# Forget logits, V's summed operands and the fourth merged splits in another order, and one gate pair computed earlier

## The chip, the cores and the metric

The kernel runs on one core of a Trainium2 chip. The metric is the device time of one execution in microseconds. TensorE (PE) multiplies, VectorE (DVE) and ScalarE (ACT) work on tiles, GpSimd (POOL) and SyncE (SP) issue DMAs here.

## The reference

One layer on x of 512 x 2048, in fp32. A normalized input is projected, three branches of attention with four heads of 128 each run on the projection, and their outputs are gated, merged and projected again:

```python
hn = rmsnorm(x, norm_g)
proj = jnp.einsum('bsd,dc->bsc', hn, w_in)        # q, k, v, SiLU gate of three branches; forget logits; merge gates
ya = forgetting_attention(qa, ka, va, f_logit)    # branch A, f_logit = 4 columns of proj + b_f
yb = chunked_relpos_attention(qb, kb, vb, rel_bias)   # branch B
yc = stick_breaking_attention(qc, kc, vc)         # branch C
ys = jnp.stack([ya, yb, yc], axis=2) * jax.nn.silu(gate)
up = jnp.einsum('bsnw,nwd->bsnd', ys, w_up)
merged = jnp.sum(sigmoid(merge_gates) * up, axis=2)
return x + jnp.einsum('bsd,de->bse', merged, w_out)
```

In branch A the forget logits go through log-sigmoid and a cumulative sum, and the differences are added to the attention logits.

## The kernel before

Every fp32 operand of a product is split in two: ACT copies it into a type of lower precision (the high part, L249) and DVE subtracts that copy to get the rest (the low part, L253). The projections then run in units of 16 matmuls on PE (L268), eight with 512 columns and eight with 256, and each unit has one tile of weights, which SP loads as `raw` and which ACT and DVE split into `w`. There are six `raw` buffers and three of `w`.

To save multiplications, blocks of the projection are computed by a scheme of seven products in place of eight, of sums of operands: products 1, 2, 6, 5, 7, 3, 4 in this order. The sums of weights are made in two ways: POOL issues a load that adds to a tile already there (L293), and DVE adds two tiles (L662, L668, and L903 for V). A pair task computes one block of q and k columns, of SiLU gates ("s"), or of merge gates ("g", a gate pair) in seven units. A value task ("v") computes the V columns of one branch in 14 units, each named (p, kh) by its product p and its half kh of the contraction. Its operands of product 1 and 5 are summed into that of product 6 (L903), and those of 2 and 6 into that of product 3. Results are gathered from the accumulators by ACT (L742, L746, L763) and DVE (L735, L750, L767, L778, L789).

The branches run as C, B, A. The first head of C has code of its own (its columns, the V task of branch C, a gate pair). For each later head the table HEADS (L1951) lists what PE computes right behind that head's q and k columns. The "v" at C's fourth head (C, 3) is V of branch B, and the "v" at B's fourth is V of branch A. In this document the three are the first, second and third V task. The heads' own softmax work lies on ACT and DVE between the splits. Small operands of attention are transposed by DMAs on SP (L281 with `tt`).

The order of everything is written out by a planner in the kernel (class Flow, L65). A task is a generator that yields an engine, a cost and, where given, a due time; the planner keeps a clock for each engine and picks the task that can start first, and among such the one due first. It runs when the program is built, and what it picks becomes the fixed order of PE, ACT, DVE, SP and POOL. So a number in a table or a due time changes the order of instructions, and each engine then works its list from the front: an instruction whose input isn't there holds all behind it.

The four places that the change touches:

- `forget_bias` (L963): the forget logits of branch A are computed early, in four partial sums, stored, loaded back as `lf_parts` in another layout by SP (L281), summed by DVE (L978), and put through some fifteen small operations (L979 to L999) with one exponential on ACT (L983). The result goes back to memory, to be loaded for the heads of branch A.
- The value task's loop over loads (L883): it sets the order in which SP loads V's weights. The loads of product 5 get POOL's accumulating load behind them. The order also shifts when DVE may make the sums (L903).
- `merged_d` (L1664): the merged output is split for the last projection in four groups m1 to m4; the fourth, `m4`, has due times of its own.
- HEADS.

Of the kernel before, what the change touches and what calls it, by code (L numbers as in the profile page):

```python
# [29 lines left out]
HS = S // 2  # L30
# [5 lines left out]
A, B, C = 0, 1, 2  # L36
# [28 lines left out]
class Flow:  # L65
# [16 lines left out]
    def give(self, slots, n=1):  # L82
        slots.free += [self.fin] * n

    def spawn(self, gen, slack, ready=None):
        task = Task(gen, slack, self.now if ready is None else ready)
        self.tasks.append(task)
        self.advance(task)
# [66 lines left out]
def act_us(n, x=1):  # L155
    return x * (0.075 + 0.00095 * n)


def dve_us(n, x=1):
    return x * (0.1 + 0.00105 * n)  # L160
# [3 lines left out]
def hybrid_kernel(  # L164
# [33 lines left out]
    flow = Flow()  # L198
# [4 lines left out]
    def t2(s, dt=F32):  # L203
        return tp.tile([P, S], dt, tag="t2", name=nm(s))
# [11 lines left out]
    def f(ap):  # L216
        return ap.bitcast(F32)
# [4 lines left out]
    LH, RH = slice(0, HS), slice(HS, S)  # L222
# [23 lines left out]
    def split(hi, lo, src, n, ev=None, due=(), hi_ev=None):  # L246

        yield (ACT, act_us(n), *due)
        nc.scalar.activation(hi, src, AF.Copy)  # L249
        if hi_ev is not None:  # L250
            set_(hi_ev)
        yield (DVE, dve_us(n), *due)
        nc.vector.tensor_sub(lo, src, f(hi))  # L253
        if ev is not None:
            set_(ev)
# [17 lines left out]
    def landing(issued, kb):  # L273

        line[0] = max(line[0], issued + 1.0) + kb / RATE
        return line[0] + 1.5

    def queued(dma, to, src, us=0.4):

        yield SP, us  # L280
        tc.keep_in_program_order(dma(to, src))  # L281

    def fetch(to, src, kb):
        yield from queued(nc.sync.dma_start, to, src)
        return Event(landing(flow.fin, kb))
# [11 lines left out]
    def added(there, begun, parts):  # L297

        yield begun
        for to, src, kb in parts:  # L300
            ev = yield from add_up(to, src, kb)
        there.t = ev.t
# [84 lines left out]
    def raw_tile(shape=(UK, P)):  # L387
        return wp.tile([P] + list(shape), F32, tag="raw", name=nm("raw"), bufs=NR)
# [230 lines left out]
    class PairTask:  # L619
# [24 lines left out]
        def load(self):  # L644
            a11, a12, a21, a22 = self.src
            for p, srcs in ((5, (a21, a22)), (1, (a11,)), (2, (a12,)), (7, (a11, a21)), (4, (a22,))):
                yield raws, 1
                t = self.w[p] = raw_tile()
                ev = yield from fetch(t, srcs[0], 512)
                if len(srcs) > 1:  # L650
                    spawn(added(self.there[p], ev, [(t, srcs[1], 512)]), 0.0, flow.fin)
                else:
                    self.there[p].t = ev.t
            self.w[6], self.w[3] = self.w[1], self.w[2]
# [165 lines left out]
    class ValueTask:  # L820
# [34 lines left out]
        def load(self):  # L855
            def src(i, kh):
                return w_v[self.n, i // 2, i % 2, kh]

            def begin(p, kh):
                if p == 7:  # L860
                    yield t2s, 2
                    self.w[p, kh] = [t2("raw").rearrange("p (j c) -> p j c", j=2) for _ in range(2)]
                else:
                    yield raws, 1
                    self.w[p, kh] = raw_tile((UK // 2, 2 * P))
                for to, c in pieces(p, kh):
                    w, kb = src({5: 2, 1: 0, 2: 1, 7: 0, 4: 3}[p], kh)[:, c], 128 * (c.stop - c.start)
                    if p == 7:
                        yield POOL, 0.8
                        tc.keep_in_program_order(nc.gpsimd.dma_start(to, w))  # L870
                        ev = Event(landing(flow.fin, kb))
                    else:
                        ev = yield from fetch(to, w, kb)
                if p in (5, 7):
                    more = [(to, src({5: 3, 7: 2}[p], kh)[:, c], 128 * (c.stop - c.start)) for to, c in pieces(p, kh)]
                    return lambda: spawn(added(self.there[p, kh], ev, more), 0.0, flow.fin)
                self.there[p, kh].t = ev.t

            def pieces(p, kh):
                w = self.w[p, kh]  # L880
                return [(w, slice(0, 4))] if p != 7 else [(t, slice(2 * i, 2 * i + 2)) for i, t in enumerate(w)]

            for p, kh in ((1, 0), (1, 1), (5, 0), (2, 0), (2, 1), (5, 1)):  # L883
                add = yield from begin(p, kh)
                if p == 5:
                    add()
            adds = []
            for kh in range(2):
                adds.append((yield from begin(7, kh)))
            for add in adds:  # L890
                add()
            for kh in range(2):
                yield from begin(4, kh)
# [69 lines left out]
    f_ev, f2_ev = Event(), Event()  # L963
    fd, fd2 = dp.tile([NQ * NH, S], F32, name="fd"), dp.tile([NH, S], F32, name="fd2")

    def forget_bias():

        T = S // 32
        lf = cp.tile([P, 4 * T], F32, name="lf")
        parts = cp.tile([P, NQ, T], F32, name="lf_parts")  # L970
        v, u, s, p = (lf[:, i * T:(i + 1) * T] for i in range(4))
        yield f_ev
        yield from queued(nc.sync.dma_start, parts,
                          fd.rearrange("(n h) (c t) -> n (h c) t", h=NH, t=T).rearrange("n c t -> c n t"))
        yield Event(f_ev.t + 12.0)
        q = 0.21
        yield DVE, 2 * q
        nc.vector.tensor_reduce(v, parts.rearrange("p n t -> p t n"), axis=AX.X, op=ALU.add)  # L978
        nc.vector.tensor_scalar_add(v, v, bfc)  # L979
        yield DVE, q  # L980
        nc.vector.scalar_tensor_tensor(u, v, -1.0, v, op0=ALU.mult, op1=ALU.min)
        yield ACT, q
        nc.scalar.activation(u, u, AF.Exp)  # L983

        yield DVE, 5 * q
        nc.vector.tensor_scalar_add(s, u, 2.0)
        nc.vector.reciprocal(s, s)
        nc.vector.tensor_mul(s, s, u)
        nc.vector.tensor_mul(u, s, s)
        nc.vector.tensor_scalar_mul(p, u, 1.0 / 17.0)  # L990
        for k in range(7, 0, -1):
            yield DVE, q
            nc.vector.scalar_tensor_tensor(p, p, 1.0 / (2 * k + 1), u, op0=ALU.add, op1=ALU.mult)
        yield DVE, 3 * q
        nc.vector.scalar_tensor_tensor(p, p, 1.0, s, op0=ALU.add, op1=ALU.mult)
        nc.vector.tensor_scalar_mul(p, p, 2.0)
        nc.vector.scalar_tensor_tensor(v, v, 0.0, p, op0=ALU.min, op1=ALU.subtract)
        yield from queued(nc.sync.dma_start, fd2.rearrange("h (c t) -> (h c) t", t=T), v)
        f2_ev.t = flow.fin + 3.0  # L999
# [474 lines left out]
    def first_head(n, h):  # L1474
        hd = Head(n, h)
        units.extend(first_quad(hd))
        at(OFF["fb"], forget_bias, 20.0)
        value_units(n)
        gate_units()
        schedule(hd, OFF["a0"], OFF["b0"])  # L1480

    def head(n, h, more, last=False):
        hd = Head(n, h, last)
        u0 = len(units)
        units.extend(PairTask(col(n, Q, h), col(n, K, h), ops, hd.got(Q), None, hd.got(K)).units)
        for i, what in enumerate(more):
            if what == "v":
                value_units(n - 1)
            elif what == "s":
                units.extend(PairTask(col(n, G, h), col(n, G, h + 1), ops, hd.got(G), None, far(n, h + 1)).units)  # L1490
            else:
                gate_units(x1_first=last and i == len(more) - 1)
        schedule(hd, u0 + 7, u0 + 21)
        return hd

    first_head(C, 0)
    for n, h, more in HEADS:
        last_head = head(n, h, more, (n, h) == (A, NH - 1))
# [107 lines left out]
    kept_m, m1_ev, up_half, up_done = {}, [Event() for _ in range(UK)], Event(), Event()  # L1606
# [47 lines left out]
    def merged_d(k, b):  # L1654

        yield up_done
        for i in range(UK):
            yield lambda: m23[i] is not None
        if k % 2 == 0:
            yield xps, 1  # L1660
            m4[k // 2] = Parts("m4")
        yield lambda: m4[k // 2] is not None
        h, lo, ev = m4[k // 2].half(k % 2)
        yield from split(h, lo, b[:, RH], HS, ev, (up_done.t + 10.0 + k,))  # L1664
        give(t2s)

    QK = UK // 4
# [265 lines left out]
    for k in range(UK):  # L1933
# [12 lines left out]
NX = 28  # L1946
NR = 6

XLATE, SLOW, RATE = 6.0, 3.0, 330.0
ONTO = {6: 1, 7: 6, 4: 7, 3: 5}  # L1950
HEADS = [(C, 1, "gg"), (C, 2, "sg"), (C, 3, "v"), (B, 0, "sggg"), (B, 1, "g"), (B, 2, "sggg"),  # L1951
         (B, 3, "gvg"), (A, 0, "sgg"), (A, 1, "gg"), (A, 2, "sggg"), (A, 3, "gggg")]

OFF = dict(cs=3, ct=12, s=11, t=17, v=1, av=8, s1=8, t1=13, v1=0, av1=3, fb=24, a0=11, b0=23)
# [55 lines left out]
```

## Time and profile before

| | before |
|---|---|
| median of 3 runs | 1295.91 us (1294.97 to 1295.99) |
| profiled execution | 1296.0 us |
| its span | 1294.3 us |
| granted TensorE clock | 1.000 |
| PE busy | 1286.4 us, 99% |
| DVE busy | 1137.5 us, 88% |
| ACT busy | 873.6 us, 67% |
| POOL busy | 100.0 us, 8% |

The span reaches from the first to the last instruction; 1.7 us lie outside it. A busy share is the mean over the span. A group's row gives its line in the kernel, the engine, the operation, output and inputs by name, the shape, and the count. Brackets behind a row give the idle time in front of it and whose end ended it.

### The profile page before, as it was taken

To read this page: it belongs to the slowest core of one execution; us is meant where nothing else is said; L and a number is where in the kernel's file an instruction comes from. 1 tells how busy PE (TensorE), PEld (TensorE's weight loads), DVE (VectorE), ACT (ScalarE), POOL (GpSimd) and SP (SyncE) were. 2 spreads that over 40 slices of the span, in tenths; PEclk is the share of its full clock that TensorE was granted. 3 is DMA by queue.
4 is the path that set the end of the run, shared out by engine and by line. 5 is a ranking of instruction groups with operands and counts; after the bars stand their busy time and mean duration, and the time that the engine had idled before them with its cause. 6 is when DMAs were issued, how large, how long until landed. Compare 5 with 4: busy or idle time off the path is not lost.

```text
span 1294.3 us, 19472 instructions
## 1 busy us (share of the span) xinstructions
PE 1286.4 (99%) x6965; PEld 1113.1 (86%) x6965; DVE 1137.5 (88%) x1667; ACT 873.6 (67%) x1359; POOL 100.0 (8%) x130
## 2 busy tenths in 40 slices
PE   9999999999999999999999999999999999999998
PEld 6888888888888888888888888888888888888887
DVE  8988889888898999989889989999899877798775
ACT  8877677778767769666867675967768655454432
POOL 0200001010110101002010000000100000000000
PEclk9999999999999999999999999999999999999999
DMA  9778798887889869889897888888979755774831
GB/s 333 232 203 217 205 233 200 210 205 194 232 228 198 236 189 220 243 190 246 203 230 209 187 229 223 210 233 190 234 203 278 239 194 195 214 235 136 247 112 65
DMA packets 130257, 274.47 MB, mean 212 GB/s; under 512 B 43104, under 2 KB 49504, under 8 KB 130160
## 3 DMA queue, kind: packets, MB, share of 16 engines
q1 hardware_dynamic: 113504, 217.19, 53.7%
q0 software_dynamic: 16224, 55.58, 25.5%
q8 instruction: 55, 0.90, 0.3%
q10 hardware_dynamic: 432, 0.45, 0.1%
q14 instruction: 42, 0.34, 0.1%
HBM read 241.54 MB, written 24.42 MB: 205 GB/s over the span
## 4 chain that ended last, share of the span: by engine, by line
PE 93%; DVE 4%; DMA 1%; issue 1%; ACT 1%; SPq 0%; ACTq 0%
PE acc L268 74%; PE att L268 14%; DVE w L253 1%; DMA sg<-gl 1%; DVE m L253 1%; PE att L264 1%; PE att L1322 1%; PE att L1323 1%; PE att L265 1%; PE att L263 1%; PE att L1321 1%; DVE sg L1586 0%; ACT w L249 0%; DMA raw<-in_w_one 0%; PE att L1435 0%
## 5 line engine op out<-in xcount | busy, mean ns | idle before, releaser
L253 DVE TENSOR_TENSOR w<-raw,w 128x1024 fp32r<-128x1024 f32 (+2 forms) x432 | 499.9, 1165 | 94.0 <-ACT w L249 93.5
L249 ACT ACTIVATE w<-raw 128x1024 fp32r<-128x1024 f32 (+2 forms) x432 | 435.2, 1011 | 216.8 <-PE att L268 106.6
L268 PE MATMUL acc<-x,w 128*128 128x512 f32 (+1 forms) x2656 | 499.7, 339 | 1.5 <-ACT v L746 1.1
L268 PEld LDWEIGHTS acc<-x,w 128*128 128x128 f32 x2656 | 424.7, 189 | 66.9 <-issue 3.4
L268 PE MATMUL acc<-t,w 128*128 128x512 f32 (+1 forms) x1920 | 357.5, 338 | 0.7 <-DVE v L767 0.7
L268 PEld LDWEIGHTS acc<-t,w 128*128 128x128 f32 x1920 | 292.6, 190 | 34.5 <-DVE v L767 0.9
L293 POOL DMA_DIRECT2D raw<-in_w_col x80 | 68.9, 861 | 785.5 <-DMA raw<-in_w_col 243.8
L268 PE MATMUL acc<-w,m 128*128 128x512 f32 x336 | 94.3, 390 | 0.5 <-DVE w L253 0.5
L268 PE MATMUL att<-w,m 128*128 128x512 f32 (+1 forms) x342 | 94.3, 385 | 0.0
L268 PE MATMUL att<-y,w 128*128 128x512 f32 x384 | 89.6, 389 | 0.0
L268 PEld LDWEIGHTS att<-y,w 128*128 128x128 f32 x384 | 72.1, 188 | 14.9
L268 PEld LDWEIGHTS acc<-w,m 128*128 128x128 f32 x336 | 63.0, 188 | 13.9 <-DVE w L253 0.9
L268 PEld LDWEIGHTS att<-w,m 128*128 128x128 f32 x342 | 63.5, 188 | 12.9
L268 PE MATMUL acc<-w,x 128*128 128x512 f32 (+1 forms) x336 | 63.0, 337 | 0.8 <-DVE w L253 0.8
L268 PEld LDWEIGHTS acc<-w,x 128*128 128x128 f32 x336 | 52.4, 190 | 7.9 <-PE att L1053 1.1
L544 DVE TENSOR_TENSOR c<-c,begin_in 128x512 f32<-128x512 f32 x80 | 54.3, 685 | 0.1
L662 DVE TENSOR_TENSOR raw<-raw,raw 128x1024 f32<-128x1024 f32 x40 | 48.8, 1220 | 0.2
L668 DVE TENSOR_TENSOR raw<-raw,raw 128x1024 f32<-128x1024 f32 x40 | 48.8, 1220 | 0.2
L742 ACT ACTIVATE u<-acc 128x512 f32<-128x512 f32 x43 | 25.5, 594 | 32.0 <-PE acc L268 31.8
L1549 ACT ACTIVATE sg<-sg,small_in 128x512 f32<-128x512 f32 x48 | 33.4, 715 | 19.9 <-DMA sg<-gl 19.8
L763 ACT ACTIVATE u<-acc 128x512 f32<-128x512 f32 x42 | 24.9, 594 | 31.6 <-PE acc L268 30.8
L268 PE MATMUL acc<-y,w 128*128 128x512 f32 x192 | 46.1, 389 | 0.0
(209 smaller groups left out, 1413.7 us busy)
## 6 DMA issues: line engine op xcount, KB each, us to landing
raw<-in_w_col SPq DMA_DIRECT2D x200, 512.0 KB, 4.7
raw<-in_w_col POOLq DMA_DIRECT2D x80, 512.0 KB, 6.4
raw<-in_w_v SPq DMA_DIRECT2D x24, 512.0 KB, 4.8
gl<-c SPq DMA_DIRECT2D x48, 256.0 KB, 3.9
raw<-in_w_up SPq DMA_DIRECT2D x32, 384.0 KB, 3.5
sg<-gl SPq DMA_DIRECT2D x48, 256.0 KB, 4.2
raw<-in_w_out SPq DMA_DIRECT2D x24, 512.0 KB, 4.5
raw<-in_w_v POOLq DMA_DIRECT2D x24, 256.0 KB, 7.6
```

The source lines that it names most:

```text
L249: nc.scalar.activation(hi, src, AF.Copy)
L253: nc.vector.tensor_sub(lo, src, f(hi))
L263: nc.tensor.matmul(ps, lh, rh, start=start, stop=False, skip_group_check=more)
L264: nc.tensor.matmul(ps, lh, rl, start=False, stop=False, skip_group_check=more)
L268: nc.tensor.matmul(ps, w, x, start=start, stop=stop, skip_group_check=more)
L293: tc.keep_in_program_order(nc.gpsimd.dma_start(to, src, accum_op=ALU.add))
L544: nc.vector.tensor_mul(c, c if src is None else src, rstd[0][:c.shape[0], :])
L662: nc.vector.tensor_add(w[1], w[1], w[5])
L668: nc.vector.tensor_add(w[2], w[2], w[1])
L742: nc.scalar.activation(self.u, ps, AF.Copy)
L763: nc.scalar.activation(self.s, ps, AF.Copy)
L1549: nc.scalar.activation(g, g, AF.Sigmoid, bias=bg[:, n * DT + d:n * DT + d + 1])
```

## The change

The load order of a V task puts the first load of product 5 right behind the first of product 1, and the second behind the first of product 2, ahead of the second of product 2. The planner's moment from which DVE may take the forget logits is now 8 us after the load of `lf_parts` was issued in the planner's clock, and no longer 12 us after the partial sums were stored. The due times of the `m4` splits are 15 us later. One gate pair moves from branch B's third head to branch C's fourth, where it stands behind that head's q and k and ahead of the second V task.

```diff
@@ -880,7 +880,7 @@
-            for p, kh in ((1, 0), (1, 1), (5, 0), (2, 0), (2, 1), (5, 1)):
+            for p, kh in ((1, 0), (5, 0), (1, 1), (2, 0), (5, 1), (2, 1)):
                 add = yield from begin(p, kh)
                 if p == 5:
                     add()
@@ -972,7 +972,7 @@
         yield from queued(nc.sync.dma_start, parts,
                           fd.rearrange("(n h) (c t) -> n (h c) t", h=NH, t=T).rearrange("n c t -> c n t"))
-        yield Event(f_ev.t + 12.0)
+        yield Event(flow.fin + 8.0)
         q = 0.21
         yield DVE, 2 * q
@@ -1661,7 +1661,7 @@
-        yield from split(h, lo, b[:, RH], HS, ev, (up_done.t + 10.0 + k,))
+        yield from split(h, lo, b[:, RH], HS, ev, (up_done.t + M4 + k,))
         give(t2s)
@@ -1946,9 +1946,10 @@
+M4 = 25.0
 XLATE, SLOW, RATE = 6.0, 3.0, 330.0
 ONTO = {6: 1, 7: 6, 4: 7, 3: 5}
-HEADS = [(C, 1, "gg"), (C, 2, "sg"), (C, 3, "v"), (B, 0, "sggg"), (B, 1, "g"), (B, 2, "sggg"),
+HEADS = [(C, 1, "gg"), (C, 2, "sg"), (C, 3, "gv"), (B, 0, "sggg"), (B, 1, "g"), (B, 2, "sgg"),
          (B, 3, "gvg"), (A, 0, "sgg"), (A, 1, "gg"), (A, 2, "sggg"), (A, 3, "gggg")]
```

The number of instructions stays the same on every engine; their order changes. Three places follow. In the rows, numbers behind a name tell buffers apart.

DVE near 105 us, before. `w<-raw` are low splits of weights, `lf` the forget logits:

```order
L253 TENSOR_TENSOR w_1170<-raw_886,w_1170 128x1024
L253 TENSOR_TENSOR w_1200<-raw_1017,w_1200 128x1024
L978 TENSOR_REDUCE lf<-lf_parts 128x16
L979 TENSOR_SCALAR lf<-lf,small_in 128x16
L981 SCALAR_TENSOR_TENSOR lf<-lf 128x16
L253 TENSOR_TENSOR w_1227<-raw_985,w_1227 128x1024
L986 TENSOR_SCALAR lf<-lf 128x16
```

DVE there, after, up to the row in front of the reduction:

```order
L253 TENSOR_TENSOR w_1200<-raw_1017,w_1200 128x1024
L253 TENSOR_TENSOR w_1227<-raw_985,w_1227 128x1024
L253 TENSOR_TENSOR w_1256<-raw_1045,w_1256 128x1024
L767 TENSOR_TENSOR v_1255<-v_1255,acc_1137 128x512
...
L253 TENSOR_TENSOR w_1331<-raw_1197,w_1331 128x1024
L1303 SCALAR_TENSOR_TENSOR y_1294<-c_692,y_1294 128x512
L978 TENSOR_REDUCE lf<-lf_parts 128x16
L979 TENSOR_SCALAR lf<-lf,small_in 128x16
```

The reduction and its successors moved behind sixteen other rows; the place of the load of `lf_parts` in SP's order is the same.

DVE at the third V task (near 590 us), before. `w_6152`, `w_6178`, `w_6203` and `w_6243` are the units (1,0), (1,1), (2,0) and (2,1), and L903 the sum of product 5's tile into product 1's:

```order
L778 TENSOR_TENSOR u_6030<-u_6030,acc_6085 128x512
L735 TENSOR_TENSOR c_913_6061<-u_6030 128x256
L253 TENSOR_TENSOR w_6152<-raw_5954,w_6152 128x1024
L259 SCALAR_TENSOR_TENSOR c_937_6192<-v_6125 128x256
...
L253 TENSOR_TENSOR w_6178<-raw_6026,w_6178 128x1024
L903 TENSOR_TENSOR raw_5954<-raw_5954,raw_6073 128x1024
L544 TENSOR_TENSOR c_937_6192<-c_937_6192,begin_in 128x512
L253 TENSOR_TENSOR sq_6120<-sa_6106,sq_6120 64x512
L253 TENSOR_TENSOR w_6203<-raw_6088,w_6203 128x1024
L253 TENSOR_TENSOR w_6243<-raw_6137,w_6243 128x1024
```

DVE there, after, with `w_6147`, `w_6180`, `w_6204` and `w_6239` as the same four units and `w_6270` as unit (6,0):

```order
L253 TENSOR_TENSOR w_6147<-raw_5935,w_6147 128x1024
L496 TENSOR_TENSOR rw_6143<-rw_6143,rv_6144 128x512
L778 TENSOR_TENSOR u_6018<-u_6018,acc_6081 128x512
L903 TENSOR_TENSOR raw_5935<-raw_5935,raw_6025 128x1024
L735 TENSOR_TENSOR c_914_6062<-u_6018 128x256
L253 TENSOR_TENSOR w_6180<-raw_6048,w_6180 128x1024
...
L253 TENSOR_TENSOR w_6204<-raw_6075,w_6204 128x1024
L1061 SCALAR_TENSOR_TENSOR rs_6141<-rs_6141,gq,c_900_5943 128x512
L253 TENSOR_TENSOR w_6239<-raw_6138,w_6239 128x1024
L903 TENSOR_TENSOR raw_6048<-raw_6048,raw_6117 128x1024
L253 TENSOR_TENSOR w_6270<-raw_5935,w_6270 128x1024
```

The split of (1,0) moved ahead of L778, the first sum ahead of (1,1)'s split, and the second sum ahead of (6,0)'s.

SP at the same place, before (`in_w_v` are V's weights):

```order
L281 DMA_TRANSPOSE tt_5785<-p_5688 128x2x128
L281 DMA_TRANSPOSE tt_5784<-p_5688 128x2x128
L281 DMA raw_5954<-in_w_v 128x1024
L281 DMA raw_6026<-in_w_v 128x1024
L281 DMA raw_6073<-in_w_v 128x1024
L281 DMA raw_6088<-in_w_v 128x1024
L281 DMA vr_6121<-vd_139 128x2x128
L281 DMA vr_6121<-vd_140 128x2x128
L281 DMA raw_6137<-in_w_v 128x1024
L281 DMA raw_6150<-in_w_v 128x1024
```

SP there, after (`raw_6025` and `raw_6117` are the two tiles of product 5):

```order
L281 DMA raw_5935<-in_w_v 128x1024
L281 DMA_TRANSPOSE tt_5957<-u_5956 128x2x128 x2
L281 DMA_TRANSPOSE tt_5958<-u_5956 128x2x128
L281 DMA_TRANSPOSE tt_5957<-p_5863 128x2x128
L281 DMA raw_6025<-in_w_v 128x1024
L281 DMA_TRANSPOSE tt_5958<-p_5863 128x2x128
...
L281 DMA raw_6048<-in_w_v 128x1024
...
L281 DMA raw_6075<-in_w_v 128x1024
...
L281 DMA raw_6117<-in_w_v 128x1024
L281 DMA raw_6138<-in_w_v 128x1024
```

The transposes of branch B's third head, which stood ahead of all six loads, now stand between them.

DVE in the output projection (near 1155 us), before. `m<-sg` are splits of `m4`, `m<-mt` of another group, and `w_11746` is the split of one unit's weights:

```order
L253 TENSOR_TENSOR w_11722<-raw_11510,w_11722 128x1024
L253 TENSOR_TENSOR m_1835_11690<-sg_10779,m_1835_11690 128x256
L253 TENSOR_TENSOR m_1833_11688<-mt_11653,m_1833_11688 128x2x256
L1752 TENSOR_TENSOR raw_11618<-raw_11618,raw_11510 128x1024
L253 TENSOR_TENSOR m_1835_11690<-sg_10916,m_1835_11690 128x256
L253 TENSOR_TENSOR m_1836_11691<-sg_11053,m_1836_11691 128x256
L253 TENSOR_TENSOR m_1836_11691<-sg_11190,m_1836_11691 128x256
L253 TENSOR_TENSOR w_11746<-raw_11709,w_11746 128x1024
```

DVE there, after, `w_11745` being the same unit:

```order
L253 TENSOR_TENSOR w_11722<-raw_11510,w_11722 128x1024
L253 TENSOR_TENSOR m_1833_11688<-mt_11653,m_1833_11688 128x2x256
L1752 TENSOR_TENSOR raw_11618<-raw_11618,raw_11510 128x1024
L253 TENSOR_TENSOR w_11745<-raw_11709,w_11745 128x1024
L253 TENSOR_TENSOR w_11763<-raw_11541,w_11763 128x1024
...
L1851 TENSOR_TENSOR o_11660<-o_11660,att_11674 128x512
L1761 TENSOR_TENSOR raw_11768<-raw_11768,raw_11409 128x1024
L253 TENSOR_TENSOR m_1834_11689<-sg_10497,m_1834_11689 128x256
```

All `m4` splits moved behind that unit's split, and behind some ten rows more.

## The prediction

> **What bounds the kernel now.** I read the page's head and busy shares first, then what TensorE (PE) waited for, then the stretches around those waits, engine by engine.
>
> ```profile
> span 1294.3 us, 19472 instructions
> PE 1286.4 (99%) x6965; PEld 1113.1 (86%) x6965; DVE 1137.5 (88%) x1667; ACT 873.6 (67%) x1359; POOL 100.0 (8%) x130
> PE 93%; DVE 4%; DMA 1%; issue 1%; ACT 1%; SPq 0%; ACTq 0%
> ```
>
> PE is busy for 99% of the span, and the chain that ended last is 93% PE. The change leaves all matmuls in place (the same number in both listings), so it can win only what PE waits, and lose only by new waits. DVE, at 88%, is the engine that can cause them. The whole list of PE's waits:
>
> ```profile
> PE acc L268 <- DVE w L253: 1.3, 2, 0.8
> PE att L1925 <- POOL nhepsc L325: 1.1, 1, 1.1
> PE acc L268 <- ACT v L746: 1.1, 1, 1.1
> PE acc L268 <- DVE v L767: 0.7, 1, 0.7
> PE acc L268 <- ACT w L414: 0.4, 1, 0.4
> ```
>
> The rows on L1925 and L414 belong to the start, which the change does not touch. The others lie at three places, and each edit of a due time or of a load order lies at one of them.
>
> **Part 1, the forget logits.** Columns: start, duration, engine, line, output<-inputs, and in brackets the idle time before and who ended it.
>
> ```profile
> 107.77 2.96 PE L268 MATMUL acc<-t,w 128*128 128x256 f32 x16
> 111.80 3.06 PE L268 MATMUL acc<-x,w 128*128 128x512 f32 x16 [1.06 <-ACT v L746]
> 115.59 3.06 PE L268 MATMUL acc<-t,w 128*128 128x256 f32 x16 [0.74 <-DVE v L767]
> 118.49 1.75 PE L268 MATMUL acc<-x,w 128*128 128x512 f32 x7
> ...
> 106.70 0.43 SPq L281 DMA_DIRECT2D lf_parts<-fd  x1
> ...
> 103.78 2.35 DVE L253 TENSOR_TENSOR w<-raw,w 128x1024 fp32r<-128x1024 f32 x2
> 110.26 0.27 DVE L978 TENSOR_REDUCE lf<-lf_parts 128x16 f32<-128x64 f32 x1 [4.12 <-DMA lf_parts<-fd]
> 110.93 1.22 DVE L253 TENSOR_TENSOR w<-raw,w 128x1024 fp32r<-128x1024 f32 x1
> 114.86 0.68 DVE L767 TENSOR_TENSOR v<-v,acc 128x512 f32<-128x512 f32 x1
> ...
> 111.04 0.22 ACT L983 ACTIVATE lf<-lf 128x16 f32<-128x16 f32 x1 [4.32 <-DVE lf L981]
> 111.16 0.58 ACT L746 ACTIVATE v<-acc 128x512 f32<-128x512 f32 x1
> ...
> L735 DVE TENSOR_TENSOR c<-u 128x256 f32<-128x256 f32 x91 | 38.3, 424 | 2.6
> ```
>
> The reduction L978 stands in DVE's order ahead of a low split. Its load, issued at 106.70, lands at 110.2, so DVE stands still for 4.12 us, ACT stands behind it at L983 for 4.32 us, and PE waits for what those two should have done. Rows of matmuls overlap each other, so the idle time in the brackets understates the loss. A unit of 16 matmuls takes 2.79 us from start to start (part 2 has two in a row without a wait, 591.59 to 597.37, with 0.2 us of other matmuls between). From 107.77 the next unit is due at 110.56 and begins at 111.80: 1.24 us. From there 114.59 is due, 115.59 seen: 1.00. Then 118.38 against 118.49: 0.11. Together 2.35 us.
>
> In the changed order sixteen DVE rows come ahead of L978. Costed by shape they are five splits and two sums (L662, L668) of 128x1024 at 1.22 as the splits above, six rows of 128x512 (L767, L778, L1303, three of L544) at 0.68 as L767, and three of 128x256 (L259, L735, L789) at 0.42 as L735 in the last row. That is 8.5 + 4.1 + 1.3 = 13.9 us, so DVE gets there no earlier than 106.1 + 13.9 = 120.0, about 9.7 us behind the landing. L983 moves on ACT from ahead of L746 to 25 rows later. The small operations of the block (15 rows of some 0.2 us) still have to run, now in pieces between splits. What hides them is the lead of the low splits: DVE had idled 4.1 us here, and it idles in front of its splits often (the row on L249 in the part on the rivals). The result goes to a scratch load for branch A's heads, and the store of it stands three places later on SP, in front of loads that have several us of lead. I cost that at nothing. Gain 2.35 us; ends: 0 if the wait moves along, 2.35 if all goes.
>
> **Part 2, the third V task.** V's unit order on PE is products 1, 2, 6, 5 and so on, two units each; T0 is its first matmul, 591.59.
>
> ```profile
> 591.59 1.07 PE L268 MATMUL acc<-w,x 128*128 128x512 f32 x4
> ...
> 597.37 0.40 PE L1053 MATMUL att<-sq,ones_r 128*128 128x512 f32 x1
> 598.58 1.62 PE L268 MATMUL acc<-w,x 128*128 128x512 f32 x6 [0.81 <-DVE w L253]
> ...
> 588.99 0.69 DVE L778 TENSOR_TENSOR u<-u,acc 128x512 f32<-128x512 f32 x1 [0.66 <-PE acc L268]
> 590.06 1.22 DVE L253 TENSOR_TENSOR w<-raw,w 128x1024 fp32r<-128x1024 f32 x1
> 593.50 1.23 DVE L253 TENSOR_TENSOR w<-raw,w 128x1024 fp32r<-128x1024 f32 x1
> 594.64 1.22 DVE L903 TENSOR_TENSOR raw<-raw,raw 128x1024 f32<-128x1024 f32 x1
> 597.21 2.36 DVE L253 TENSOR_TENSOR w<-raw,w 128x1024 fp32r<-128x1024 f32 x2
> ...
> 567.15 2.47 SPq L281 DMA_TRANSPOSE tt<-p  x2
> ...
> 575.26 0.33 SPq L281 DMA_DIRECT2D raw<-in_w_v  x1
> ...
> 580.24 0.33 SPq L281 DMA_DIRECT2D raw<-in_w_v  x1
> ...
> 584.17 0.86 POOL L293 DMA_DIRECT2D raw<-in_w_v  x1 [13.61 <-DMA raw<-in_w_v]
> 593.49 0.90 POOL L293 DMA_DIRECT2D raw<-in_w_v  x1 [0.75 <-DMA raw<-in_w_v]
> ...
> raw<-in_w_v POOLq DMA_DIRECT2D x2, 512.0 KB, 6.9
> ```
>
> Unit (2,0) is due at 591.59 + 2 x 2.79 + 0.43 (two matmuls of L1053) = 597.60 and starts at 598.58: 0.98 us, and its successor is 0.08 later still. It waits for the low split that begins at 597.21. That split comes late because DVE stood at L778 for a PE product with the split of (1,0) behind it; (1,0)'s ended only at 591.2, 0.4 us ahead of T0, and the rest follow in a row.
>
> In the changed order the split of (1,0) stands ahead of L778, and the sum of (5,0) into (1,0) follows. By durations from T0: L778 begins at T0 - 2.6 (588.99), then 0.68 + 1.22 + 0.42 + 1.22 put the end of (1,1)'s split at T0 + 1.0 to 1.2, needed after T0 + 2.8. L789, two of L544, one of L498 (0.68, a row of that shape) and the split of (2,0) end at T0 + 4.5, needed at T0 + 5.6: 1.1 us to spare. L1061 (0.7) and (2,1) end at T0 + 6.3, needed at T0 + 8.8. So the wait goes, 1.06 us.
>
> Two covers have to hold. The sum stands on DVE ahead of (1,1)'s split, so the accumulating load of (5,0) must have landed by T0 + 0.8. Before, it was issued at 584.17 and took some 6.9 us (T0 - 0.5); with (5,0) second in SP's queue instead of third its load leaves, by my estimate near T0 - 14: the second load left at 575.26 (T0 - 16.3) and the third at 580.24 (T0 - 11.4), and two transposes of 1.2 us more stand ahead of the second now, so the add lands near T0 - 3. The second sum, of (5,1) into (1,1), now stands ahead of (6,0)'s split: before, (5,1)'s add was issued at 593.49 and landed near 600.4 = T0 + 8.8; the new order asks it by T0 + 8.8 too (needed T0 + 11.2, less sum and split at 2.4). As (5,1) is now fifth of six and not sixth, I expect T0 + 8.1: 0.7 us to spare. Both ends for this term: 1.06 gained, or nothing.
>
> The Trainium skill, "DMA: Bandwidth & Descriptors", section "Anatomy of one DMA — SWDGE (gpsimd) path", fits such a load as 2.0 us + bytes/436e3, an estimate of 3.2 us for 512 KB. By that the add would land 3.7 us earlier and the second cover would be wide; the trace does not agree, with 6.9 us here, and it decides, so the cover counts as thin.
>
> **Part 3, the fourth merged splits.**
>
> ```profile
> 1154.88 1.07 PE L268 MATMUL att<-w,m 128*128 128x512 f32 x4
> 1156.42 0.73 PE L268 MATMUL acc<-w,m 128*128 128x512 f32 x2 [0.47 <-DVE w L253]
> ...
> 1154.14 1.09 DVE L253 TENSOR_TENSOR m<-sg,m 128x256 fp32r<-128x256 f32 x3
> 1155.15 1.22 DVE L253 TENSOR_TENSOR w<-raw,w 128x1024 fp32r<-128x1024 f32 x1
> ```
>
> Due at 1154.88 + 0.91 (four matmuls) = 1155.79, seen at 1156.42: 0.63, and 0.11 after. DVE did six of the eight m4 splits ahead of the w split PE waited for, the last three in the row at 1154.14; at some 0.34 each that is 2.0 us. In the new order all eight stand behind it, and it ends near 1156.3 - 2.0 = 1154.3, 1.5 us ahead of need. m4 is first used some 45 us later (by counting PE's matmuls on), and eight rows of 0.34 us fit into that. Gain 0.74; ends 0 and 0.74.
>
> **Part 4, the gate pair moved.** It costs no extra matmul. Its seven units (19.5 us) go ahead of the second V task, which so moves under branch C's last scores; after branch B's third head it is missing, and the third V task loses nothing of its lead. All orders between about 150 and 720 us change.
>
> ```profile
> 262.00:722.00 460.00, 459.19 (x2643) 405.79 (x2643) 413.22 (x590) 333.64 (x515) 45.57 (x54) 1.00 0.86 215
> DVE w L253 <- ACT w L249: 93.5, 102, 4.5
> ```
>
> Columns are length, then busy PE, PEld, DVE, ACT, POOL. PE lacks 0.8 us there, the wait of part 2 alone. A new order of the same 460 us has 165 units, each a chance for a wait; DVE's 413 us leave 10%, and DVE waits 102 times for a high split, so it is usually early. Following DVE's new rows under the second V task with the durations above, I find 1.0 us to spare at its tightest units ((5,0), (7,0)) and 0.8 at (6,0) if the second add lands as late as above. I take 0.2 us; ends 0 and 4.
>
> **The sum.** 2.35 + 1.06 + 0.74 = 4.15, less 0.2 = 3.95. The profiled execution is 1296.0 (span and 1.7 outside it), so 1292.05; the median of the runs is 1295.91, 0.1 below, so 1292.0.
>
> **The rivals.** *A wait re-forms inside a V task.* For it: the 0.7 and 0.8 us to spare rest on one add's duration; against: (2,0) is 1.1 clear. Price 0.6 to 1.1 us: 1292.5 to 1293.1.
>
> *The moved rows do not free what they should.* The forget block's small rows meet other late work 10 us on, or the sixteen rows move faster than I sum. Price 0.7 to 2.35 us: 1292.7 to 1294.3. Against it: L978 is 9.7 us behind its landing.
>
> *The new order of the heads brings several small waits* among 165 units, at 0.5 to 1 us each: four of them return all the gain, 1293.7 to 1296.
>
> *Slower: SP's queue at the third V task.* Ten transposes of branch B's third head (1.2 us each) now stand between V's loads; before, all of them had gone first. They wait for that head's softmax. If they hold (5,0)'s load past T0 - 10 (its add needed at T0 + 0.8, less the add's 6.9 and the 3.9 from load to add, 580.24 to 584.17), DVE stops at the sum with (1,1)'s split behind it, and each us later is a us of PE. To be slower by 0.2% it must eat 3.95 + 2.6 = 6.6 us, a load at T0 - 3.4, nine transposes late against my T0 - 14: 1298.6 and more. Against it: in the rows of part 2 the two transposes at 567.15 run back to back, so SP did not wait for that softmax there.
>
> **How the numbers follow.** 0.2%, 2.6 us, is about what a measurement of this kernel can tell from no change. Forecast 0.44 (1291.5 to 1292.4, faster); a V wait 0.24 (0.20 faster, 0.04 same); moved rows 0.10 (0.06 faster, 0.04 same); small waits 0.14 (same); SP 0.08 (slower). Faster 0.70, same 0.22, slower 0.08. The range leaves out the slower case and the upper part of the small waits: 1291.2 to 1294.5.
>
> **What would show it.** Right: no 4 us of DVE idle at L978; PE's list without L746 and L767, and without L253 near 598 and 1156; PE idle after the start under 0.5 us. Wrong: PE idle on L253 within V's units at (6,0) with POOL or DVE L903 behind it; L903 idle on an `in_w_v` add; SP transposes ending within 10 us of T0; or PE waits strewn over 260 to 720 us.

## The result, and the profile after

The changed kernel took 1291.99 us (median of 6 executions, 1291.00 to 1292.51) against 1295.95 for the kernel before: a ratio of 0.9969, 95% interval 0.9959 to 0.9979, or about 4.0 us faster. The forecast was 1292.0. Measured once more beside other kernels, in 11 executions, the same program took 1293.34 us (1291.44 to 1296.95; ratio 0.998, 0.9971 to 0.9989). Both intervals lie below 1; all 17 executions together have a median of 1292.25. The second set is much wider than the first, and most of what follows is about why.

Of the page after, the head, the busy shares and the shares of the chain that ended last:

```profile
span 1290.3 us, 19475 instructions
PE 1285.5 (100%) x6965; PEld 1113.2 (86%) x6965; DVE 1138.8 (88%) x1667; ACT 874.0 (68%) x1359; POOL 100.0 (8%) x130
PE 97%; DMA 1%; SPq 0%; DVE 0%; ACT 0%; issue 0%; ACTq 0%; POOLq 0%
```

The counts of the five engines are those of the kernel before; the three instructions more in the head are semaphore instructions, which are not counted as busy.

All that PE waited for in the changed kernel, by line (total us, times, longest):

```profile
PE att L1925 <- POOL nhepsc L325: 1.1, 1, 1.1
PE acc L268 <- ACT w L414: 0.2, 1, 0.2
```

The rows on L746, L767 and L253 are gone; what stands here belongs to the start. The three places, in order of time.

PE at the forget logits in the changed kernel (start, duration, engine, line, what it does, count):

```profile
107.75 2.96 PE L268 MATMUL acc<-t,w 128*128 128x256 f32 x16
110.55 2.93 PE L268 MATMUL acc<-x,w 128*128 128x512 f32 x16
113.31 2.96 PE L268 MATMUL acc<-t,w 128*128 128x256 f32 x16
116.11 5.72 PE L268 MATMUL acc<-x,w 128*128 128x512 f32 x32
```

Units follow each other every 2.8 us without a break. DVE reaches the reduction much later and does not stand there:

```profile
121.29 0.27 DVE L978 TENSOR_REDUCE lf<-lf_parts 128x16 f32<-128x64 f32 x1
121.59 0.23 DVE L979 TENSOR_SCALAR lf<-lf,small_in 128x16 f32<-128x16 f32 x1
```

In the output projection PE runs through where it had waited at 1156.42:

```profile
1151.61 1.07 PE L268 MATMUL att<-w,m 128*128 128x512 f32 x4
1152.52 0.61 PE L268 MATMUL acc<-w,m 128*128 128x512 f32 x2
1152.97 0.62 PE L268 MATMUL att<-w,m 128*128 128x512 f32 x2
```

At the third V task T0, its first matmul, is now 589.41. PE there, with the split of (1,0) long done:

```profile
589.41 1.07 PE L268 MATMUL acc<-w,x 128*128 128x512 f32 x4
...
594.07 1.07 PE L268 MATMUL att<-w,x 128*128 128x512 f32 x4
594.98 5.73 PE L268 MATMUL acc<-w,x 128*128 128x512 f32 x32
600.82 1.19 PE L268 MATMUL acc<-w,t 128*128 128x512 f32 x4
```

The wait at (2,0), which begins at 594.98, is gone. But (6,0), due at T0 + 4 x 2.79 = 600.57, starts at 600.82, and one matmul behind it lags by 0.11 more. By the rows PE is idle for only 0.11 us there, too short for the list above. The chain of work that released it, followed back (start, duration, what; SPq is SP's queue of transfers):

```profile
578.72 1.19 SPq L281
...
579.96 2.29 SPq L281
...
582.30 1.39 SPq L281
...
583.79 6.50 DMA raw<-in_w_v
...
590.83 5.94 DMA raw<-in_w_v
596.77 0.02 issue
596.79 1.24 DVE raw L903
...
598.13 0.13 ACT w L249
598.26 0.84 issue
599.10 0.67 ACT rv L488
599.77 0.52 ACT rt L492
600.29 0.49 ACT u L742
600.78 0.04 issue
600.82 0.50 PE acc L268
```

In words: three transposes on SP, which run from 578.72 to 583.69, the load of (5,1) behind them at 583.79, POOL's add to it at 590.83, DVE's second sum at 596.79, ACT's high split of that sum (the unit (6,1)), two small ACT operations, and then L742, which takes a product's result out of the accumulators that (6,0) needs. The price in this execution is 0.4 us. Summed over all matmuls, the time by which a start lies later than its unhindered interval fell from 10.7 to 6.9 us. Of the 3.8, 2.35 are the forget logits, 0.74 the m4 splits, and 1.06 - 0.39 the third V task; nothing else is larger than 0.2 us at one place. The span is 4.0 us shorter; the last 0.2 us are not placed.

### The profile page after: what moved, and what is told of

Its sections match the earlier page's. It is cut to its first block, busy times and chain, and to the rows that moved or that the text cites. A ratio compares the mean times of both kernels' runs of the same rounds, so it can differ in the third digit from the quotient of the medians.

```text
span 1290.3 us, 19475 instructions
## 1 busy us (share of the span) xinstructions
PE 1285.5 (100%) x6965; PEld 1113.2 (86%) x6965; DVE 1138.8 (88%) x1667; ACT 874.0 (68%) x1359; POOL 100.0 (8%) x130
## 4 chain that ended last, share of the span: by engine, by line
PE 97%; DMA 1%; SPq 0%; DVE 0%; ACT 0%; issue 0%; ACTq 0%; POOLq 0%
PE acc L268 76%; PE att L268 17%; DMA raw<-in_w_v 1%; PE att L264 1%; PE att L1322 1%; PE att L1323 1%; PE att L265 1%; PE att L263 1%; PE att L1321 1%; SPq L281 0%; DMA raw<-in_w_one 0%; PE att L1435 0%; PE att L1053 0%; DVE raw L903 0%; DVE w L253 0%
## 5 line engine op out<-in xcount | busy, mean ns | idle before, releaser
L253 DVE TENSOR_TENSOR w<-raw,w 128x1024 fp32r<-128x1024 f32 (+2 forms) x432 | 501.0, 1166 | 94.7 <-ACT w L249 93.6
L742 ACT ACTIVATE u<-acc 128x512 f32<-128x512 f32 x43 | 25.6, 595 | 32.8 <-PE acc L268 32.6
```

The lines of the kernel that those rows point to most:

```text
L742: nc.scalar.activation(self.u, ps, AF.Copy)
```

## The experiments

All are compared with the kernel before, 1295.8 to 1295.9 us in each set. The three sets ran on different chips, each with the kernel before beside it. Each experiment's short name stands in brackets.

**Each edit alone.** The forget logits alone (forget_only):

```diff
-        yield Event(f_ev.t + 12.0)
+        yield Event(flow.fin + 8.0)
```

> The kernel before with the moment of the forget logits alone. Theory (PE's wait is all that the edit is worth): the waits on L746 and L767 are gone from PE's list, DVE does not stand at L978, PE's other waits (0.8 on L253 near 598 us, 0.5 near 1156) stay; 1295.95 - 2.35 = 1293.6 us. Rival (the small rows of the block only carry the lateness 10 us on): part of the 2.35 us returns as PE waits on L253 or L746 between 120 and 160 us; 1294.5 us or more.

Measured 1293.38 us (1292.23 to 1295.60, 11 executions), ratio 0.9981 (0.9972 to 0.9989): 2.4 us faster. The theory holds; PE's list there has no row on L746 or L767, and keeps the other two waits:

```profile
PE acc L268 <- DVE w L253: 1.1, 2, 0.8
PE att L1925 <- POOL nhepsc L325: 1.1, 1, 1.1
PE acc L268 <- ACT w L414: 0.9, 1, 0.9
```

The load order alone (vorder_only):

```diff
-            for p, kh in ((1, 0), (1, 1), (5, 0), (2, 0), (2, 1), (5, 1)):
+            for p, kh in ((1, 0), (5, 0), (1, 1), (2, 0), (5, 1), (2, 1)):
```

> The kernel before with the load order of the V tasks alone. Theory A (the wait at the third V task comes from the split of (1,0) standing behind L778, and this edit leaves that row where it is): the wait of about 1 us near 598 us stays, and since L903 now stands ahead of (1,1)'s split it may grow by up to 0.5 us; 1295.7 to 1296.5 us. Theory B (the load order is what frees the split of (2,0)): the wait is gone; 1295.95 - 1.06 = 1294.9 us.

Measured 1297.08 us (1296.01 to 1298.00), ratio 1.0006 (0.9998 to 1.0015), so no gain and perhaps a loss. Theory A holds and was still too friendly. PE at the third V task of this kernel:

```profile
596.75 1.19 PE L268 MATMUL acc<-w,x 128*128 128x512 f32 x4 [0.20 <-DVE w L253]
...
599.42 0.92 PE L268 MATMUL acc<-w,x 128*128 128x512 f32 x3 [0.32 <-DVE w L253]
```

The old wait of 0.98 has become two, 0.36 and 0.49 by their starts, because the first sum now stands ahead of (1,1)'s split. New are 0.6 us at 66.7 us, in the first V task, and 0.3 at 313 us. The first of these is no net loss: PE began that task 0.95 us earlier than in the profile before, and the unit that waits, (6,0), begins at 66.67 us here and at 66.87 there.

The later m4 splits alone (m4_only):

```diff
-        yield from split(h, lo, b[:, RH], HS, ev, (up_done.t + 10.0 + k,))
+        yield from split(h, lo, b[:, RH], HS, ev, (up_done.t + 25.0 + k,))
```

> The kernel before with the later due times of the m4 splits alone. Theory: PE's wait near 1156 us is gone and none comes in the last 150 us; 1295.95 - 0.74 = 1295.2 us. Rival (the splits are late where m4 is first used, near 1203 us, or push another split late): a new PE wait after 1156 us, 1295.9 us or more.

Measured 1295.45 us (1294.24 to 1297.01), ratio 0.9993 (0.9985 to 1.0002). The time alone can't tell 0.7 us from nothing. The profile can: no wait stands near 1156 us nor after it. The same execution had a wait of 0.7 us at 339 us, where the order is that of the kernel before, so executions differ by as much as this edit is worth. The wait itself differs as well. In profiles with the old due times PE loses 0.75 us at that place before, 0.85 in vorder_only, 0.56 in forget_only, 0.38 in heads_only and nothing in heads_vorder.

The moved gate pair alone (heads_only):

```diff
-HEADS = [(C, 1, "gg"), (C, 2, "sg"), (C, 3, "v"), (B, 0, "sggg"), (B, 1, "g"), (B, 2, "sggg"),
+HEADS = [(C, 1, "gg"), (C, 2, "sg"), (C, 3, "gv"), (B, 0, "sggg"), (B, 1, "g"), (B, 2, "sgg"),
```

> The kernel before with the moved gate pair alone. Theory A (the moved pair is what puts the split of (1,0) ahead of L778 at the third V task): the wait near 598 us is gone, 1.06 us, and what comes new between 262 and 720 us is 0 to 0.7 us; 1294.9 to 1295.6 us. Theory B (the move costs small waits and gains nothing): the wait near 598 us stays and 0.2 us come on top; 1296.1 us.

Measured 1295.97 us (1294.57 to 1299.53), ratio 1.0001 (0.9993 to 1.0009). Theory A is right on the place and wrong on the sum. The wait at (2,0) is gone with this edit and without the load order. In its stead the second sum comes late. DVE and PE of this kernel, T0 being 591.1:

```profile
602.94 1.23 DVE L903 TENSOR_TENSOR raw<-raw,raw 128x1024 f32<-128x1024 f32 x1 [2.68 <-DMA raw<-in_w_v]
...
605.38 0.74 PE L268 MATMUL acc<-w,t 128*128 128x256 f32 x4 [0.20 <-ACT w L249]
...
607.89 1.21 PE L268 MATMUL acc<-w,t 128*128 128x512 f32 x4 [1.30 <-DVE w L253]
```

DVE stands 2.7 us for the add of (5,1), which is loaded last here, and the unit (6,1) pays 0.36 + 1.46 us. So the gate pair removes one wait and makes another of at least that size.

**Edits taken together and apart.** The first is the changed kernel with the old load order (all_but_vorder):

> The changed kernel with the old load order of the V tasks. Theory A (with the gate pair moved, product 5's second tile in the sixth slot of the loads comes too late: its load took 9.9 us and its add 5.6 in heads_only, and DVE stood 2.7 us at L903 for it): the same 1.8 us of PE waits at the units (6,1) and (7,0) of the third V task in place of the 0.39 us that the changed kernel has at (6,0); 1292.0 - 0.4 + 1.8 = 1293.4 us. Theory B (that late load was one execution's chance): no wait there over 0.5 us; 1291.6 to 1292.1 us.

Measured 1294.01 us (1292.63 to 1297.17), ratio 0.9986 (0.9977 to 0.9994). Theory A: its profile shows the same waits, now 0.82 and 1.46 us, with DVE standing 3.06 us at the second sum. So the late load was not one execution's chance.

The gate pair and the load order, without the other two edits (heads_vorder):

> The kernel before with the moved gate pair and the new load order, without the other two edits. Theory A (the two need each other: the pair takes the wait at (2,0) of the third V task away, the load order keeps it from coming back at its later units): 1295.9 - 1.06 + 0.39 = 1295.2 us, with the waits on L746 and L767 near 112 and 115 us and on L253 near 1156 us as before. Theory B (edits add up: alone they were measured +0.2 and +1.3 us): 1297.4 us.

Measured 1296.65 us (1293.37 to 1298.67), ratio 1.0001 (0.9992 to 1.0010). The median lies between the theories, nearer to B, and the spread of 5 us is larger than either. Its profiled execution shows how the order of instructions that costs 0.4 us at the third V task of the changed kernel can cost 3.7 there. PE, then DVE:

```profile
604.50 1.20 PE L268 MATMUL acc<-w,t 128*128 128x512 f32 x4 [1.91 <-ACT u L742]
605.54 1.67 PE L268 MATMUL att<-w,t 128*128 128x512 f32 x4
607.01 1.05 PE L268 MATMUL acc<-w,t 128*128 128x256 f32 x4
...
600.47 1.22 DVE L903 TENSOR_TENSOR raw<-raw,raw 128x1024 f32<-128x1024 f32 x1 [2.75 <-DMA raw<-in_w_v]
```

It is the same chain, with the add landed at T0 + 9.2 (T0 is 591.30) and not at T0 + 7.4. And after the wait four matmuls that take 1.07 us elsewhere take 1.67. There the granted clock is lower. Of the same execution, the columns are the stretch, its length, busy PE, PEld, DVE, ACT and POOL (each with its count), the granted clock, the DMA share and GB/s:

```profile
605.00:606.00 1.00, 1.00 (x6) 0.82 (x5) 1.00 (x3) 0.92 (x2) 0.00 (x0) 0.90 1.12 193
606.00:607.00 1.00, 1.00 (x3) 0.72 (x3) 1.00 (x2) 0.00 (x0) 0.00 (x0) 0.50 1.09 254
607.00:608.00 1.00, 1.00 (x6) 0.99 (x5) 1.00 (x2) 0.00 (x0) 0.00 (x0) 0.50 0.92 373
608.00:609.00 1.00, 1.00 (x7) 1.00 (x6) 1.00 (x2) 0.05 (x1) 0.00 (x0) 0.50 0.31 70
609.00:610.00 1.00, 1.00 (x9) 1.00 (x9) 0.86 (x2) 1.00 (x2) 0.00 (x0) 0.90 0.96 319
```

Half the clock for some 3.4 us (605.8 to 609.2 in finer stretches), by which the unit (6,0) and the start of the next take 1.7 us longer. The wait is the only idle time of PE near it, and up to 1290 us the clock is at 1.00 in every other microsecond of this profile. That the wait caused the drop is likely from this, but no experiment shows it.

Only the second tile of product 5 earlier, ((1,0), (1,1), (5,0), (2,0), (5,1), (2,1)), with the other three edits (second_swap):

> The changed kernel with the load order (1,0), (1,1), (5,0), (2,0), (5,1), (2,1): only the second tile of product 5 is loaded earlier. Theory A (it is this tile's add that binds): no wait over 0.5 us at the third V task; 1291.6 to 1292.3 us. Theory B (the first tile's place matters as much): DVE stands at the first L903 with the split of (1,1) behind it, and PE waits 0.5 us or more at (2,0); 1292.5 us or more.

Measured 1292.32 us (1291.03 to 1294.40, 6 executions), ratio 0.9974 (0.9962 to 0.9985). The median lies at the upper end of theory A's range (1292.3). Its condition, no wait over 0.5 us, does not hold in the one profiled execution, 1294.24 us and at the slow end, which still has 0.39 us at (6,1) and 0.84 at the unit behind it, where DVE had stood 1.1 us for the second tile's add; and 0.69 us at (2,0) of the second V task, where DVE stood 1.98 us at the first sum with (1,1)'s split behind it, as theory B said of the third. In this execution both tiles matter, each at another task.

Only the first tile earlier, ((1,0), (5,0), (1,1), (2,0), (2,1), (5,1)), with the other three edits (first_swap):

> The changed kernel with the load order (1,0), (5,0), (1,1), (2,0), (2,1), (5,1): only the first tile of product 5 is loaded earlier; in DVE's order the second sum L903 still stands ahead of the split of (6,0). Theory A (the second tile's add binds): in heads_only the add of a sixth load landed 11.8 us behind the first matmul of the task; sum and split add 2.3, (6,0) is needed at 11.2, so PE waits some 2 to 3 us at (6,0); 1293.6 to 1294.6 us. Theory B: as the changed kernel, 1292.0 us.

Measured 1297.21 us (1295.09 to 1299.90), ratio 1.0013 (1.0004 to 1.0022): slower than the kernel before, with the gains of the forget logits and of m4 in it. Theory A had the mechanism and too small a price; the profiled execution, the fastest, waits 3.4 us at (6,0) by its start, with a full clock:

```profile
603.86 1.21 PE L268 MATMUL acc<-w,t 128*128 128x512 f32 x4 [3.22 <-ACT u L742]
```

The ten others were at mean clocks of 0.997 to 0.999 and took 1295.95 to 1299.90, that is 0.9 to 4.8 us more than the profiled one. As an estimate from these numbers, a clock short by 0.001 to 0.003 over 1295 us loses 1.3 to 3.9 us, so a lower clock can be most of what they took more. None of them was profiled, so that stays an estimate.

The changed kernel again (after_again):

> The changed kernel once more, beside the others. Theory A (the third V task's second sum has 0 to 2 us of slack by how long SP's sixth-slot loads and POOL's add take, and one profile caught it at 0.4 us of wait): executions spread over 3 us or more, 1291 to 1296 us, and the median is 1292.0 to 1293.0. Theory B (the 1291.0 to 1292.5 us of its six executions are its whole spread): median 1291.8 to 1292.2, none over 1293.

Measured 1293.34 us, 1291.44 to 1296.95: theory A, with a median 0.3 above its range. The profiled execution waits 2.0 us at (6,0), by the same chain. PE and DVE of it, and the load and the add from its chain, T0 being 589.59:

```profile
602.73 1.19 PE L268 MATMUL acc<-w,t 128*128 128x512 f32 x4 [1.84 <-ACT u L742]
...
598.69 1.23 DVE L903 TENSOR_TENSOR raw<-raw,raw 128x1024 f32<-128x1024 f32 x1 [2.69 <-DMA raw<-in_w_v]
...
583.92 7.13 DMA raw<-in_w_v
...
591.60 7.07 DMA raw<-in_w_v
```

From the sum's start to PE's are 4.04 us here and 4.03 in the first profile (596.79 to 600.82). What differs is the add's landing: T0 + 7.4 there, T0 + 9.1 here. The load left at the same distance from T0 (5.6 and 5.7 us ahead of it). It took 0.6 us more than in the first profile (7.13 against 6.50), and the add 1.1 us more (7.07 against 5.94).

The forget logits and m4 alone (fm_only):

> The kernel before with the forget logits and the m4 splits alone: neither the gate pair nor the load order is touched. Theory A (these two are independent and carry most of the gain): 1295.9 - 2.35 - 0.74 = 1292.8 us, with PE's wait of 0.98 us near 596 us left. Theory B (the gate pair and the load order are needed for the gain): 1293.5 us or more.

Measured 1293.19 us (1292.12 to 1297.03), ratio 0.9981 (0.9972 to 0.9990). Theory A, 0.4 us short: the two independent edits bring 2.7 of the 3.1 us expected. Their profile keeps one wait on the splits, 0.98 us at 596 us. This is as fast as the changed kernel in the same set.

The changed kernel without the moved gate pair (all_but_heads):

> The changed kernel without the moved gate pair. Theory A (the load order alone does not help the third V task, and brings small waits as in vorder_only: 0.36 + 0.49 there against 0.98 before, 0.3 to 0.5 at the second task): 1292.8 + 0.3 = 1293.1 us, at most 1294. Theory B (it helps as soon as the other two edits are in): 1292.0 us or less.

Measured 1296.19 us (1294.38 to 1299.88), ratio 1.0002 (0.9994 to 1.0011). Neither theory: the load order without the gate pair costs 3.0 us against fm_only. Its profiled execution, 1294.38 us, is 1.6 us behind fm_only's, 1292.74. Matmul by matmul, 0.7 us of this arises at the second V task (264 to 267 us), 0.4 near 312 and 0.3 near 338 us. The third V task's two waits (0.36 and 0.48 us) cost as much as fm_only's single one of 0.98, and the first V task's 0.5 us only uses up a lead. The executions near 1297 to 1300 were not profiled, and the rest of the 3.0 us stays open.

A load order with the second tile of product 5 one place earlier than in the change (early_51):

```diff
-            for p, kh in ((1, 0), (5, 0), (1, 1), (2, 0), (5, 1), (2, 1)):
+            for p, kh in ((1, 0), (5, 0), (1, 1), (5, 1), (2, 0), (2, 1)):
```

> The changed kernel with the load order (1,0), (5,0), (1,1), (5,1), (2,0), (2,1): the second tile of product 5 is loaded one place earlier still, the first of product 2 one later. Theory A (the second sum binds at the third V task by its add): the add lands some 4 us earlier, the wait on L742 at (6,0) is gone, what is left is the split of (2,0), whose load now lands near T0 + 1.5 with 1.6 us to spare; 1291.6 us and a narrower spread than the changed kernel. Theory B (product 2's load takes its place as what comes late): a wait of 0.5 us or more at (2,0), 1292.3 us or more.

Measured 1291.79 us (1291.30 to 1292.94, 6 executions), ratio 0.9970 (0.9959 to 0.9981), beside 1293.34 for the changed kernel in the same set. Theory A. SP's load, POOL's add, DVE's sum and PE at the unit, T0 being 590.65:

```profile
579.38 0.52 SPq L281 DMA_DIRECT2D raw<-in_w_v  x1
...
588.31 0.86 POOL L293 DMA_DIRECT2D raw<-in_w_v  x1 [6.48 <-DMA raw<-in_w_v]
...
595.18 1.22 DVE L903 TENSOR_TENSOR raw<-raw,raw 128x1024 f32<-128x1024 f32 x1
...
596.21 5.73 PE L268 MATMUL acc<-w,x 128*128 128x512 f32 x32
601.78 1.07 PE L268 MATMUL acc<-w,t 128*128 128x512 f32 x4
```

The sum starts at T0 + 4.5 without standing, and (6,0) starts 5.57 us behind the two units before it: no wait, in the second or the third V task. The profiled execution, 1292.87 us, loses 2.0 us between 55 and 68 us against the first profile of the changed kernel: 1.3 us around a wait on ACT's L1415, which no other profile has, and 0.7 us around (6,0) of the first V task. It had come there 0.7 us ahead. Whether the new order has a part in that is not known. The intervals of the two ratios overlap, and the changed kernel's first six executions had 0.9969, so it is not shown that this order beats the changed kernel.

## Why the prediction was right, and where it was not

*The forget logits, 2.35 us.* Right in place, mechanism and size: 2.4 us measured alone, 1.75 to 2.5 us lost at that place in the five profiles of kernels without this edit, L978 reached at 121.3 (120.0 was given as the earliest), and no wait carried along.

*The m4 splits, 0.74 us.* Right by the trace, where the wait goes and none follows. The time of whole executions gives 0.35, with an interval from 1.9 faster to 0.3 slower. The 0.74 was the loss of one execution; the five profiles with the old due times lose 0 to 0.85 us there, 0.5 in the mean, so the term was perhaps some 0.2 too large.

*The third V task, 1.06 us less 0.2.* The wait at (2,0) went as worked out, and what it rested on held ((1,1) and (2,0) were on time, and the first sum found its add landed, with a load at 573.11, T0 - 16.3, against T0 - 14 estimated). Two things failed. The prediction did not say which edit does it, and in its reading of the place the new load order stood first; it is the gate pair (heads_only against vorder_only), and the load order only repairs, in part of the executions, what the gate pair breaks. And the step "the new order asks it by T0 + 8.8 too" was wrong. It followed DVE's row for (6,0)'s split. What binds is ACT: the high split of (6,1) stands ahead of L742 in ACT's list, waits for the same sum, and L742 frees the accumulators of (6,0). From the landing to PE's start are 4.05 us, so the add was asked by T0 + 11.16 - 4.05 = T0 + 7.1, and the "0.7 us to spare" were, at the expected T0 + 8.1, 1.0 us of wait. The measured landings, T0 + 7.4 and T0 + 9.1, give waits of 0.3 and 2.0. In the first profile a landing 0.7 us earlier than expected hid most of the error of 1.7 us in the need. By the chain, SP's queue set when the load left: three transposes stand in front of it.

So the first rival, a wait that re-forms in a V task, is what happens in both profiles of the changed kernel. Its price of 0.6 to 1.1 us was too narrow (0.4 and 2.0 seen, and 3.7 in heads_vorder, where the clock fell). Its chance of 0.24 looks low as well: 8 of the 17 executions lie at or above 1292.5, where its range begins, though only one of the eight was profiled.

*The gate pair's new order, 0.2 us.* No other wait came between 150 and 720 us in either profile of the changed kernel; the second V task's 0.8 to 1.0 us held there, and fell only with the load orders tried above. What the prediction left out is that the load order is that of the first V task too. A wait of 0.5 to 0.6 us near 67 us appears in five of seven profiled executions of kernels that load (5,0) second; of the seven others two have 0.2 and 0.3. That the order costs time there is not shown. DVE's rows up to the split of (6,0) stand in the same order in the kernel before, and in four of the five (6,0) begins at 66.62 to 66.88 us, against 66.87 before without a wait. PE had begun that task 0.6 to 0.95 us earlier in these four, and the wait uses up that lead.

*The other rivals.* The moved rows freed what they should. SP's transposes did not hold the first tile of product 5 back, so the slower case did not come about in the changed kernel; but that queue is how the second tile comes late: the three transposes from 578.72 to 583.69 stand directly ahead of its load, in the chain of both profiles. In first_swap the loss that rival described, DVE standing at a sum with what PE needs behind it, is real, at the other sum.

*The signs.* Two of the signs that were to show the prediction wrong stand in the first profile of the changed kernel, though its time is the one forecast: DVE stands 0.95 us at L903 for an `in_w_v` add, and SP's transposes end at 583.69, 5.7 us ahead of T0.

*The sum.* 3.95 us were forecast and 3.96 measured first. That agreement to the tenth is luck: the second set of the same program gave 2.5. Against fm_only the two edits at the V tasks gave between 1.3 us gain (first set) and 0.15 loss (same set), and without the other two edits (heads_vorder) no gain, where 0.86 was forecast. So that term is not confirmed. The total comes out near the forecast since the forget logits and m4 are 3.1 of the 3.95, and these two alone measured 2.7.

The durations of load and add decided the thin cover. In the changed kernel's two chains the add took 5.94 and 7.07 us, in heads_vorder's 6.48 (593.97 to 600.45), on the side of the profile's 6.9. The estimate of 3.2 us from the fit of the Trainium skill, "DMA: Bandwidth & Descriptors", section "Anatomy of one DMA — SWDGE (gpsimd) path", is about half of that; the trace again lies above it, with the DMA engines 94% busy between 575 and 600 us of the changed kernel.

## What to carry to other kernels

Where a late transfer is released through several in-order engines, follow each engine's list to the last thing that the bound engine needs, not only the row that reads like its operand: here an unrelated copy on ACT, behind a split that waited for the transfer, set the need 1.7 us earlier than DVE's row did. Where a cover depends on a DMA of 6 to 7 us and is under 2 us wide, one profile does not tell its cost; try to give it slack by issuing the transfer one slot earlier (here the wait was gone in the one profile taken), and take several executions. And edits in a written-out order are not additive: beside the two sure edits, the load order alone cost 3.0 us by the medians and the gate pair alone 0.8 (within the noise), and both together gave between a gain of 1.3 and a loss of 0.15.

## What the runs showed of the hardware

In one execution (heads_vorder) the granted clock fell to 0.50 from 605.8 to 609.2 us, 1.3 us behind the end of a wait of 2.07 us on PE, which cost 1.7 us on top. A wait of 3.4 us in first_swap and one of 2.0 in the changed kernel were followed by a clock of 1.00. So waits of about the same length did not cost the same in each execution. The Trainium skill, "TensorE: Matmul & The Clock Gate", section "Part 1: The HAM clock gate (the "warmup" mystery)", has the clock at half after an idle window of about 3.4 us that runs free of the kernel. The length of the slow stretch, 3.4 us, and the dependence on chance agree with that. But PE's idle time here, 1.91 us, was shorter than one window, so if this wait is the cause, a wholly idle window is not needed.
